# Bidirectional DeltaNet scan on one core: the inverse's product in the other PSUM bank, output sums one step later, square-root chains as steps of VectorE's list

## The chip, the cores and the metric

The kernel runs on one core of one Trainium2 chip. The metric is device time in microseconds (us) of one execution, taken as the median of several runs. A core has TensorE (PE; its weight loads are listed apart as PEld), VectorE (DVE), ScalarE (ACT), GpSimd (POOL) and SyncE (SP, which issues the DMAs here). PSUM is the memory that TensorE writes its products to; this kernel uses it in tiles of 128 partitions x 512 fp32, one bank each.

## What is computed

One encoder layer over 1024 tokens and 16 learned ones, width 1024, in fp32:

```
h = rmsnorm(x, norm1_w); proj = h @ w_in
q, k, v, z, b, a, sc_b, sc_c, sc_x, gate_a, gate_b = split(proj)
o   = gated_deltanet_bidir(q, k, v, z, b, a, ...)          # 8 heads, d = 128, forward + backward scan
y_a = o @ w_branch_dn
y_b = (sc_b * dwconv3(sc_c * sc_x)) @ w_branch_sc
x  += (sigmoid(gate_a) * y_a + sigmoid(gate_b) * y_b) @ w_out
x  += (silu(h2 @ w_gate) * (h2 @ w_up)) @ w_down           # h2 = rmsnorm(x, norm2_w)
out = rmsnorm(x, final_norm_w)
```

The scan of one head and one direction, chunk after chunk (S is a 128 x 128 state, carried from step to step):

```
def step(S, inp):
    v_new = u_c - w_c @ S
    o_c   = qd_c @ S + qk_c @ v_new
    S     = S * gl_c + kd_c.T @ v_new
```

with `u` and `w` from a triangular solve within each chunk. The outputs of both directions are summed, and then scaled by an inverse root of their mean square.

## The kernel before, in words

The work falls into two stages. The first holds the input projection (8 heads x q, k, v, the short convolution's columns, the gates and z), the convolutions and all of the DeltaNet. The second holds the branch projections, the output projection and the SwiGLU; the change does not touch it.

In the first stage the instruction order of every engine is written out by the kernel itself. The main loop emits the dense projections as single matmuls (`dense_steps`, line 340: three products in a split-fp32 format for each of 8 blocks of the contraction). After each of them it calls `run_streams()` and `pump()`. `run_streams` advances four generators, one each for the decay matrices (`g_decay`), the key products (`g_norm`), the inverse of the chunk's triangular matrix (`g_inv`) and the scan (`g_scan`). A generator yields the time at which it wants to go on. It works these times out in a small planner: `T` holds a clock for each engine, `pe(ns)`, `V(n)` and `A(n)` add what an instruction should cost there, and a stream goes on when `T["pe"]` has reached the time it yielded. So between two products of a scan step there stand as many dense matmuls as the planner thinks are needed to cover the work of VectorE and ScalarE in between. `pump` hands single VectorE instructions out of three lists (`conv`: convolutions, `fs`: the forward substitution of `g_inv`, `norm`: the root chains) while VectorE's clock is at most 700 ns ahead of TensorE's. The engines run what they get strictly in that order; the waits between them are semaphores that are put in from the tiles and banks that the instructions touch. One lock (`take`) keeps the scan and the last part of `g_inv` out of each other's three PSUM banks (`pss`, the `pd` tiles of the profile).

One head has one scan of NC = 8 steps. Step i works on chunk i forwards (d = 0) and on chunk 7 - i backwards (d = 1). It takes two banks, `b1` and `b2`, of four 128 x 128 places each:

- line 806: `b1[:, d]` = kT . S, then line 809: `b2[:, d]` = qT . S (TensorE);
- line 816: `r0[d]` = v - decay . `b1[:, d]` (VectorE);
- line 821: `b1[:, 2 + d]` = NP . r0, the product with the inverse (TensorE);
- lines 828 and 833: `w[d]` and `v2[d]`, two scaled copies each of `b1[:, 2 + d]` (ScalarE);
- line 838: `b1[:, d]` = kn . w over the first product's place (TensorE; not in the last step);
- line 842: `b2[:, 2 + d]` = PQ . v2 (TensorE);
- line 851: the new S from `b1[:, d]` (VectorE);
- lines 860 to 880: the output of each direction into `oacc[c]`. In steps 0 to 3 the chunk is met for the first time: a ScalarE copy of `b2[:, d]` (line 869; line 865 where there is no state yet), then a VectorE sum with `b2[:, 2 + d]` (line 875). In steps 4 to 7 a VectorE multiply and add (line 872), the sum (line 875), and a square with its sum over the row on ScalarE (line 879). Direction 0 comes first in all of it, then direction 1.

Ahead of step 0 the learned tokens give the first state (lines 788 to 796, with the VectorE scaling of line 791 and the product of line 793). After step 7 the function `norm` works out the inverse roots with `rsqrt` (line 141 onwards, eleven small VectorE instructions of 9 columns, lines 145 to 155) and scales the outputs (line 891). The same chain for the keys is `norm_job`. Both put the eleven instructions into VectorE's queue in one go.

Of the kernel before, what the change touches and what calls it, by code (L numbers as in the profile page):

```python
# [8 lines left out]
F32 = mybir.dt.float32  # L9
# [7 lines left out]
P = 128  # L17
# [30 lines left out]
def encoder_layer(ctx: ExitStack, tc: tile.TileContext, x, meta, norm1_w, w_in, w_ba,  # L48
# [225 lines left out]
    def V(n, kind=0):  # L274
        return on("dve", (68 + 1.042 * n, 130 + 1.042 * n, 130 + 0.52 * n)[kind])

    def A(n):
        return on("act", 144 + 0.834 * n)
# [209 lines left out]
    def fs_job(h, fN, fP):  # L488

        for j in range(31):  # L490
# [9 lines left out]
            V(r * n)  # L500
            yield T["dve"] + DEP

    def norm_job(st_, ssk1, cc, ce, he, y, tmp, sk):
        nc.vector.tensor_tensor(out=ce, in0=cc, in1=he, op=ALU.mult)
        V(18)
        yield T["dve"] + DEP
        rsqrt(y, ssk1, tmp)
        [V(9) for _ in range(11)]
        yield T["dve"] + DEP
        nc.vector.tensor_tensor(out=sk, in0=y, in1=ssk1, op=ALU.mult)  # L510
        V(9)

# [244 lines left out]
    def g_scan(h, st_):  # L757
        nonlocal freed
        kq, vT, small, kn, NP, PQ, Pm = (st_[k] for k in ("kq", "vT", "small", "kn", "NP", "PQ", "Pm"))
        kT, qT = kq[:, 0], kq[:, 1]  # L760
        ssk, ssq, rk2, ssk1, y, tmp, sk = (small[:, :, i] for i in range(7))
        cc, ce = small[:, :, 7:9], small[:, :, 9:11]
        sso = small[:, :, 11]
        vS = dn.tile([P, 9, P], F32, tag="vS", name=uid("vS"))
        yield from take("scan")

        def newbank():
            return pss().rearrange("p (a n) -> p a n", a=4)

        for grp in ((8, 0, 7), (1, 2, 3), (4, 5, 6)):  # L770
            pt = newbank()
            for i, c in enumerate(grp):
                if c == 8:
                    transpose(pt[:META, i], vT[:, 0:META])
                else:
                    transpose(pt[:, i], vT[:, cs(c)])
            yield pe(330)
            for i, c in enumerate(grp):
                p = META if c == 8 else P
                nc.scalar.activation(vS[:p, c], pt[:p, i], AF.Copy, scale=sk[:p, c:c + 1])  # L780
                A(P)
        yield T["act"] + HOP

        oacc = [NP[:, c, c // 4] for c in range(NC)]


        bank = newbank()
        mm(bank[:META, 0], Pm, vS[:META, 8], start=True, stop=True)
        yield pe(215)
        w = dn.tile([P, P], F32, tag="w0", name=uid("w"))  # L790
        nc.vector.tensor_scalar(out=w[:META], in0=bank[:META, 0], scalar1=ce[:META, 8, 0:1], scalar2=None, op0=ALU.mult)
        yield V(P, 1)
        mm(bank[:, 1], kn[:META, 8], w[:META], start=True, stop=True)
        yield pe(215)
        S0 = dn.tile([P, P], F32, tag="S0", name=uid("S"), bufs=2)
        nc.vector.tensor_copy(S0, bank[:, 1])
        yield V(P, 1)
        S = [S0, None]
        seen = set()
        for i in range(NC):  # L800
            cd = (i, NC - 1 - i)
            hd = (h, 8 + h)
            act_ = [d for d in range(2) if S[d] is not None]
            b1, b2 = newbank(), newbank()
            for d in act_:
                mm(b1[:, d], kT[:, cs(cd[d])], S[d], start=True, stop=True)
            t = pe(215 * len(act_))
            for d in act_:
                mm(b2[:, d], qT[:, cs(cd[d])], S[d], start=True, stop=True)
            pe(215 * len(act_))  # L810
            yield t
            r0 = [vS[:, cd[0]], vS[:, cd[1]]]
            for d in act_:
                c = cd[d]
                r0[d] = dn.tile([P, P], F32, tag=f"r{d}", name=uid("r0"))
                nc.vector.scalar_tensor_tensor(out=r0[d], in0=b1[:, d], scalar=negEG[:, c, hd[d]:hd[d] + 1], in1=vS[:, c],
                                               op0=ALU.mult, op1=ALU.add)
                t = V(P, 1)
            yield t
            for d in range(2):  # L820
                mm(b1[:, 2 + d], NP[:, cd[d], d], r0[d], start=True, stop=True)  # L821
            yield pe(430)
            w = [None, None]
            v2 = [None, None]
            for d in range(2):
                c = cd[d]
                w[d] = dn.tile([P, P], F32, tag=f"w{d}", name=uid("w"))
                nc.scalar.activation(w[d], b1[:, 2 + d], AF.Copy, scale=ce[:, c, d:d + 1])  # L828
                t = A(P)
            for d in range(2):  # L830
                c = cd[d]
                v2[d] = dn.tile([P, P], F32, tag=f"v2{d}", name=uid("v2"))
                nc.scalar.activation(v2[d], b1[:, 2 + d], AF.Copy, scale=cc[:, c, d:d + 1])
                tv = A(P)
            if i < NC - 1:
                yield t
                for d in range(2):
                    mm(b1[:, d], kn[:, cd[d]], w[d], start=True, stop=True)  # L838
                t = pe(430)
            yield tv  # L840
            for d in range(2):
                mm(b2[:, 2 + d], PQ[:, cd[d], d], v2[d], start=True, stop=True)
            t2 = pe(430)
            if i < NC - 1:
                yield t
                for d in range(2):
                    Sn = dn.tile([P, P], F32, tag=f"S{d}", name=uid("S"), bufs=2)
                    if S[d] is None:
                        nc.vector.tensor_copy(Sn, b1[:, d])
                    else:  # L850
                        nc.vector.scalar_tensor_tensor(out=Sn, in0=S[d], scalar=eGl[:, cd[d], hd[d]:hd[d] + 1],  # L851
                                                       in1=b1[:, d], op0=ALU.mult, op1=ALU.add)
                    t = V(P, 1)
                    S[d] = Sn
            else:
                freed += 1
                yield t2

            for d in range(2):
                c = cd[d]  # L860
                eg = eG[:, c, hd[d]:hd[d] + 1]
                first = c not in seen
                seen.add(c)
                if d not in act_:
                    nc.scalar.copy(oacc[c], b2[:, 2 + d])
                    A(P)
                    continue
                if first:
                    nc.scalar.activation(oacc[c], b2[:, d], AF.Copy, scale=eg)
                    A(P)  # L870
                else:
                    nc.vector.scalar_tensor_tensor(out=oacc[c], in0=b2[:, d], scalar=eg, in1=oacc[c],
                                                   op0=ALU.mult, op1=ALU.add)
                    V(P, 1)
                nc.vector.tensor_tensor(out=oacc[c], in0=b2[:, 2 + d], in1=oacc[c], op=ALU.add)
                V(P)
                if not first:
                    jk = dn.tile([P, P], F32, tag="jk", name=uid("jk"))
                    nc.scalar.activation(jk, oacc[c], AF.Square, accum_out=sso[:, c:c + 1])
                    on("act", 310)  # L880
            yield t


        def norm():
            nc.vector.tensor_scalar(out=ssq, in0=ssq, scalar1=EPS, scalar2=EPS * P, op0=ALU.add, op1=ALU.mult)
            nc.vector.scalar_tensor_tensor(out=sso, in0=sso, scalar=1.0 / P, in1=ssq, op0=ALU.mult, op1=ALU.add)
            rsqrt(y, sso, tmp)
            [V(9) for _ in range(13)]
            yield T["dve"] + DEP
            for c in range(NC):  # L890
                nc.vector.tensor_scalar(out=oacc[c], in0=oacc[c], scalar1=y[:, c:c + 1], scalar2=None, op0=ALU.mult)
                V(P, 2)
                yield T["dve"] + DEP
        lock["scan"] = None
        yield T["act"] + HOP
        job = enqueue("norm", norm())
        while not job.done:
            yield T["pe"] + 300
        yield T["dve"] + HOP
        for c4 in range(2):  # L900
            oT = NP[:, 4 * c4:4 * c4 + 4, 1 - c4]
            pt = newbank()
            for c in range(4):
                transpose(pt[:, c], oacc[4 * c4 + c])
            yield pe(430)
            nc.scalar.copy(oT, pt)
            A(512)
            nc.sync.dma_start(o_d[h][:, c4 * 512:(c4 + 1) * 512].rearrange("p (c t) -> p c t", c=4), oT)
# [868 lines left out]
```

## Time and profile before

| | |
|---|---|
| time, median of 3 runs | 2029.02 us (2028.56 to 2034.96) |
| the profiled execution | 2032.53 us |
| its span, first to last instruction | 2030.8 us |
| granted TensorE clock | 0.998 |
| TensorE busy | 2001.7 us, 99% of the span |
| VectorE busy | 1349.6 us, 66% |
| ScalarE busy | 821.3 us, 40% |
| GpSimd busy | 122.8 us, 6% |

The profile is one execution. Its views are: the page; the groups of instructions by line; the waits (who waited for whom: total us, times, longest); one line's instructions; and the timeline, in which a row gives the start in us, the duration in us, the engine, the line, the operation, output<-inputs and, in brackets, how long the engine was idle before it and what ended that. Matmul ends are modelled, so a product's row can reach into the next one's; the starts are recorded. Each fp32 product of the scan shows as two matmul rows (high and low part), hence x4 for a pair.

### The profile page before, as it was taken

Reading aid. Unit: us, or ns where it says so; the run is one execution under the profiler, and the core shown is the slowest. Engines: PE = TensorE matmul, PEld = TensorE weight load, DVE = VectorE, ACT = ScalarE, POOL = GpSimd, SP = SyncE. Lnnn points to the kernel's source line nnn. Section 1 sums busy time; section 2 is a strip of 40 time slices with the busy share of each in tenths; the row PEclk is TensorE's granted clock in tenths of the full one; section 3 lists DMA queues with packets and bytes.
Section 4 is the critical chain, followed back from the end, with each engine's and each line's share of the span. In section 5 each row is a group of like instructions: output and inputs, shape, how many; then the busy total and the mean of one; then the engine's idle time right before and its main releaser. Section 6 shows DMA issues by size and latency. Waiting matters only on the chain.

```text
span 2030.8 us, 31965 instructions
## 1 busy us (share of the span) xinstructions
PE 2001.7 (99%) x12059; PEld 1726.3 (85%) x12059; DVE 1349.6 (66%) x2966; ACT 821.3 (40%) x1945; POOL 122.8 (6%) x407
## 2 busy tenths in 40 slices
PE   9999999999999999999999999999999999999998
PEld 8998898989898988787888888887888888888887
DVE  6888577888888888663214534458867566656575
ACT  6471353645454545534213212134333333335344
POOL 2002102020202020200000000000000000000000
PEclk9999999999999999999999999999999999999999
DMA  3121222222122122221326733122755354477654
GB/s 141 64 69 58 64 85 57 74 59 73 59 68 64 66 66 78 85 89 58 99 99 209 246 122 128 52 83 99 254 207 218 137 174 166 158 275 244 194 174 167
DMA packets 131409, 247.85 MB, mean 122 GB/s; under 512 B 45045, under 2 KB 54694, under 8 KB 128823
## 3 DMA queue, kind: packets, MB, share of 16 engines
q1 hardware_dynamic: 130679, 244.77, 36.4%
q8 instruction: 94, 1.54, 0.3%
q10 hardware_dynamic: 576, 1.05, 0.1%
q14 instruction: 60, 0.49, 0.1%
HBM read 179.10 MB, written 66.67 MB: 121 GB/s over the span
## 4 chain that ended last, share of the span: by engine, by line
PE 49%; DVE 2%; DMA 1%; ACT 1%; issue 0%; SPq 0%; DVEq 0%; ACTq 0%
PE pd L1517 10%; PE pm L340 6%; PE pe L1517 4%; PE pm L1517 3%; PE pe L135 1%; PE pe L133 1%; PE pe L134 1%; PE pd L135 1%; PE pd L133 1%; PE pd L134 1%; PE pe L1685 1%; PE pe L1684 1%; PE pe L1683 1%; PE pd L1685 1%; PE pd L1684 1%; PE pd L1683 1%
## 5 line engine op out<-in xcount | busy, mean ns | idle before, releaser
L340 PE MATMUL pm<-hTh,wl 128*128 128x512 f32 (+4 forms) x1424 | 495.9, 353 | 0.7 <-DVE wl L944 0.7
L340 PE MATMUL pm<-hTh,wh 128*128 128x512 f32 (+4 forms) x1424 | 495.7, 353 | 0.8 <-ACT ra L433 0.4
L340 PE MATMUL pm<-al,wh 128*128 128x512 f32 (+4 forms) x1424 | 495.5, 353 | 0.0
L340 PEld LDWEIGHTS pm<-hTh,wh 128*128 128x128 f32 x1424 | 266.8, 188 | 19.9 <-issue 1.1
L340 PEld LDWEIGHTS pm<-hTh,wl 128*128 128x128 f32 x1424 | 267.1, 188 | 19.0 <-DVE wl L944 1.9
L340 PEld LDWEIGHTS pm<-al,wh 128*128 128x128 f32 x1424 | 267.0, 188 | 16.9
L944 DVE TENSOR_TENSOR wl<-raw,wh 128x512 fp32r<-128x512 f32 x134 | 90.5, 689 | 84.0 <-ACT wh L947 83.6
L101 DVE TENSOR_TENSOR al<-raw,ring_h 128x1024 fp32r<-128x1024 f32 x73 | 88.8, 1223 | 65.2 <-ACT ring_h L100 64.9
L100 ACT CAST ring_h<-raw 128x1024 fp32r<-128x1024 f32 x73 | 76.8, 1053 | 106.8 <-PE pd L1685 35.3
L362 DVE SCALAR_TENSOR_TENSOR kq<-ra,wc,kq 128x520 f32<-128x520 f32 x128 | 96.9, 757 | 10.7 <-ACT kq L392 8.3
L947 ACT CAST wh<-raw 128x512 fp32r<-128x512 f32 x134 | 78.6, 620 | 13.2 <-PE pm L340 9.6
L100 ACT CAST wh<-raw 128x1024 fp32r<-128x1024 f32 x43 | 45.2, 1050 | 85.8 <-PE pe L134 34.5
L495 DVE TENSOR_TENSOR tm<-fP,fN 128x135 f32<-128x135 f32 (+23 forms) x248 | 72.4, 292 | 4.2
L499 DVE TENSOR_TENSOR fP<-fP,tm 128x135 f32<-128x135 f32 (+23 forms) x248 | 71.9, 290 | 4.6
L828 ACT ACTIVATE w<-pd,small 128x128 f32<-128x128 f32 x128 | 40.1, 365 | 82.0 <-PE pd L821 67.0
L1519 DVE TENSOR_TENSOR b<-pd,b 128x512 f32<-128x512 f32 x22 | 15.2, 690 | 68.3 <-PE pd L1517 68.3
L1620 ACT ACTIVATE b<-b 128x512 f32<-128x512 f32 x22 | 13.9, 632 | 115.0 <-DVE b L1519 115.0
L101 DVE TENSOR_TENSOR wl<-raw,wh 128x1024 fp32r<-128x1024 f32 x43 | 52.4, 1220 | 11.1 <-ACT wh L100 10.9
L665 POOL TENSOR_TENSOR tm<-mP,mN 1x15 f32<-1x15 f32 (+7 forms) x120 | 44.5, 371 | 203.3 <-DMA mN<-ndm 194.8
L851 DVE SCALAR_TENSOR_TENSOR S<-S,eGl,pd 128x128 f32<-128x128 f32 x104 | 31.6, 342 | 36.1 <-PE pd L838 18.1
L1517 PE MATMUL pd<-b_hl,wh 128*128 128x512 f32 x176 | 54.3, 390 | 0.0
L533 ACT ACTIVATE PQ<-PQ,negG 128x128 f32<-128x128 f32 x128 | 43.0, 394 | 17.8 <-DVE PQ L528 17.8
(523 smaller groups left out, 4426.5 us busy)
## 6 DMA issues: line engine op xcount, KB each, us to landing
raw<-in_w_in_dram SPq DMA_DIRECT2D x72, 512.0 KB
raw<-in_w_gate_up_dram SPq DMA_DIRECT2D x44, 512.0 KB
sums<-in_w_down_dram SPq DMA_DIRECT2D x22, 512.0 KB
t_d<-sums SPq DMA_DIRECT2D x11, 1024.0 KB
raw<-s_d SPq DMA_DIRECT2D x44, 256.0 KB
raw<-t_d SPq DMA_DIRECT2D x44, 256.0 KB
act_d<-b SPq DMA_DIRECT2D x43, 256.0 KB
raw<-act_d SPq DMA_DIRECT2D x33, 256.0 KB
```

Source lines behind the costliest of these rows:

```text
L100: nc.scalar.copy(hi, src)
L101: nc.vector.tensor_tensor(out=lo, in0=src, in1=hi.bitcast(F32), op=ALU.subtract)
L133: mm(po[:m, :n], wh[:, k, :m], xhk[:, t0:t0 + n], start=(k == 0), stop=False)
L340: mm(po[:, :n], ww[:, k], f(k)[:, t0:t0 + n], start=i == 0, stop=i == 3 * KT - 1)
L362: nc.vector.scalar_tensor_tensor(out=acc, in0=raw[:, h0 + t:h0 + t + hn], scalar=wc[:, t, col:col + 1], in1=acc, op0=ALU.mult, op1=ALU.add)
L495: nc.vector.tensor_tensor(out=tv, in0=fP[:, 0:r, j:j + 1].broadcast_to([P, r, n]), in1=fN[:, j:j + 1, j + 1:32].broadcast_to([P, r, n]), o ...
L499: nc.vector.tensor_tensor(out=fP[:, 0:r, j + 1:32], in0=fP[:, 0:r, j + 1:32], in1=tv, op=ALU.subtract)
L533: nc.scalar.activation(PQ[:, c, d], PQ[:, c, d], AF.Exp, bias=negG2[:, c, hd:hd + 1])
L665: nc.gpsimd.tensor_tensor(out=tv, in0=mP[:, 0:j + 1, j:j + 1].broadcast_to([1, j + 1, n]), in1=mN[:, j:j + 1, j + 1:META].broadcast_to([1, ...
L944: nc.vector.tensor_tensor(out=u[1][1][:, k], in0=u[2][:, k], in1=u[1][0][:, k].bitcast(F32), op=ALU.subtract)
L947: nc.scalar.copy(u[1][0][:, k], u[2][:, k])
L1517: mm(po, x[:, k], y, start=k + i == 0 and not add_to, stop=k == 3 and i == 2, skip_group_check=add_to)
```

## The change

The product with the inverse goes to `b2[:, 2 + d]`, the place that PQ . v2 takes later in the same step; `w` and `v2` are copied from there. The code of the outputs becomes a function. At the end of a step it issues only the copies (or multiply-adds) of `b2[:, d]`, for both directions one after the other. The sums with `b2[:, 2 + d]`, and the squares behind them, are kept in a list and issued in the next step, straight behind the two `r0` instructions; those of the last step follow after a yield behind it. The root chains become a generator that hands out one VectorE instruction at a time, each with a cost and a ready time in the planner; the two instructions ahead of the chain in `norm` are handed out singly too. The arithmetic and the numbers of instructions are the same.

```
+    def rsqrt_steps(y, a, tmp):
+        v = nc.vector
+        ops = [lambda: v.tensor_scalar(out=y.bitcast(I32), in0=a.bitcast(I32), scalar1=1, scalar2=None, op0=ALU.logical_shift_right),
+               lambda: v.tensor_scalar(out=y.bitcast(I32), in0=y.bitcast(I32), scalar1=-1, scalar2=0x5F3759DF,
+                                       op0=ALU.mult, op1=ALU.add)]
+        ops += 3 * [lambda: v.tensor_tensor(out=tmp, in0=y, in1=y, op=ALU.mult),
+                    lambda: v.scalar_tensor_tensor(out=tmp, in0=tmp, scalar=-0.5, in1=a, op0=ALU.mult, op1=ALU.mult),
+                    lambda: v.scalar_tensor_tensor(out=y, in0=tmp, scalar=1.5, in1=y, op0=ALU.add, op1=ALU.mult)]
+        for f in ops:
+            f()
+            V(9)
+            yield T["dve"] + DEP
 ...
-        rsqrt(y, ssk1, tmp)
-        [V(9) for _ in range(11)]
-        yield T["dve"] + DEP
+        yield from rsqrt_steps(y, ssk1, tmp)
 ...
+        pending = []
+        def outputs():
+            while pending:
+                pending.pop(0)()
+
+        def output(b2, c, d, sums):
+            eg = eG[:, c, (h, 8 + h)[d]:(h, 8 + h)[d] + 1]
+            first = c not in seen
+            seen.add(c)
+            if not sums:
+                nc.scalar.copy(oacc[c], b2[:, 2 + d])
+                A(P)
+                return
+            if first:
+                nc.scalar.activation(oacc[c], b2[:, d], AF.Copy, scale=eg)
+                A(P)
+            else:
+                nc.vector.scalar_tensor_tensor(out=oacc[c], in0=b2[:, d], scalar=eg, in1=oacc[c],
+                                               op0=ALU.mult, op1=ALU.add)
+                V(P, 1)
+            def add_up():
+                nc.vector.tensor_tensor(out=oacc[c], in0=b2[:, 2 + d], in1=oacc[c], op=ALU.add)
+                V(P)
+                if not first:
+                    jk = dn.tile([P, P], F32, tag="jk", name=uid("jk"))
+                    nc.scalar.activation(jk, oacc[c], AF.Square, accum_out=sso[:, c:c + 1])
+                    on("act", 310)
+            pending.append(add_up)
 ...
+            outputs()
             yield t
             for d in range(2):
-                mm(b1[:, 2 + d], NP[:, cd[d], d], r0[d], start=True, stop=True)
+                mm(b2[:, 2 + d], NP[:, cd[d], d], r0[d], start=True, stop=True)
 ...
-                nc.scalar.activation(w[d], b1[:, 2 + d], AF.Copy, scale=ce[:, c, d:d + 1])
+                nc.scalar.activation(w[d], b2[:, 2 + d], AF.Copy, scale=ce[:, c, d:d + 1])
 ...
-                nc.scalar.activation(v2[d], b1[:, 2 + d], AF.Copy, scale=cc[:, c, d:d + 1])
+                nc.scalar.activation(v2[d], b2[:, 2 + d], AF.Copy, scale=cc[:, c, d:d + 1])
 ...
             for d in range(2):
-                c = cd[d]
-                eg = eG[:, c, hd[d]:hd[d] + 1]
 ...
-                nc.vector.tensor_tensor(out=oacc[c], in0=b2[:, 2 + d], in1=oacc[c], op=ALU.add)
-                V(P)
 ...
+                output(b2, cd[d], d, d in act_)
             yield t
+        yield t2
+        outputs()
 ...
         def norm():
             nc.vector.tensor_scalar(out=ssq, in0=ssq, scalar1=EPS, scalar2=EPS * P, op0=ALU.add, op1=ALU.mult)
+            V(9)
+            yield T["dve"] + DEP
             nc.vector.scalar_tensor_tensor(out=sso, in0=sso, scalar=1.0 / P, in1=ssq, op0=ALU.mult, op1=ALU.add)
-            rsqrt(y, sso, tmp)
-            [V(9) for _ in range(13)]
+            V(9)
             yield T["dve"] + DEP
+            yield from rsqrt_steps(y, sso, tmp)
```

More of the change, by code (lines that the diff above doesn't have):

```diff
@@ L859, in g_scan @@
             for d in range(2):
-                c = cd[d]
-                eg = eG[:, c, hd[d]:hd[d] + 1]
[L862 to L875, printed above, removed]
-                V(P)
[L877 to L880, printed above, removed]
+                output(b2, cd[d], d, d in act_)
             yield t
+        yield t2
+        outputs()
         def norm():
             nc.vector.tensor_scalar(out=ssq, in0=ssq, scalar1=EPS, scalar2=EPS * P, op0=ALU.add, op1=ALU.mult)
+            V(9)
+            yield T["dve"] + DEP
             nc.vector.scalar_tensor_tensor(out=sso, in0=sso, scalar=1.0 / P, in1=ssq, op0=ALU.mult, op1=ALU.add)
-            rsqrt(y, sso, tmp)
-            [V(9) for _ in range(13)]
+            V(9)
             yield T["dve"] + DEP
+            yield from rsqrt_steps(y, sso, tmp)
             for c in range(NC):
```

## The prediction

> **What bounds the kernel now.** I read the page first, then the main product's line, then the waits, and then the timeline of single scan steps.
>
> ```profile
> span 2030.8 us, 31965 instructions
> ...
> PE 2001.7 (99%) x12059; PEld 1726.3 (85%) x12059; DVE 1349.6 (66%) x2966; ACT 821.3 (40%) x1945; POOL 122.8 (6%) x407
> ...
> L340 PE MATMUL pm<-hTh,wh x1424: 302/334/586, 16.3 to 1081.7; 128*128 128x512 f32 x58, 128*128 128x320 f32 x40, 128*128 128x384 f32 x40, 128*128 128x336 f32 x24
> ...
> L891 DVE TENSOR_SCALAR NP<-NP,small x64: 277/281/289, 278.7 to 974.2; 128x128 f32<-128x128 f32 x64
> ```
>
> TensorE sets the time. Its first stage, where the scans run, reaches to the last dense product at 1081.7 us. The last head's outputs are scaled at 974.2, so the streams end 107 us before their cover does. What the change can give or cost is therefore TensorE time lost in waits of that stage. The waits that bear on the edited lines:
>
> ```profile
> ACT jk L879 <- DVE NP L875: 67.7, 57, 3.0
> ...
> PEld pd L838 <- ACT v L833: 17.5, 45, 0.6
> ...
> DVE NP L875 <- ACT NP L869: 15.3, 39, 0.5
> ...
> PEld pd L821 <- DVE r L816: 8.0, 18, 1.0
> ...
> PEld pd L793 <- DVE w L791: 2.9, 5, 1.0
> ...
> PE pd L821 <- DVE r L816: 2.6, 7, 0.7
> ...
> PE pe L590 <- DVE PQ L617: 2.1, 4, 0.8
> ...
> PE pd L793 <- DVE w L791: 1.5, 4, 0.7
> ...
> L838 PE MATMUL pd<-w,kn 128*128 128x128 f32 x224 | 39.0, 297 | 3.2 <-ACT v L833 0.5
> ...
> L821 PE MATMUL pd<-r,NP 128*128 128x128 f32 x240 | 38.8, 281 | 2.9 <-DVE r L816 2.6
> ```
>
> The telling row is the second: the product kn.w (line 838) reads `w` and never `v`, yet its weight load waits 45 times for the copies into `v`. Here is one step in order of time, from the sums of the step before to PQ.v2:
>
> ```profile
> 441.42 0.28 DVE L875 TENSOR_TENSOR NP<-pd,NP 128x128 f32<-128x128 f32 x1
> ...
> 441.74 0.37 ACT L869 ACTIVATE NP<-pd,eG 128x128 f32<-128x128 f32 x1 [0.50 <-DVE NP L875]
> ...
> 442.14 0.29 DVE L875 TENSOR_TENSOR NP<-pd,NP 128x128 f32<-128x128 f32 x1 [0.44 <-ACT NP L869]
> ...
> 442.35 0.31 DVE L495 TENSOR_TENSOR tm<-fP,fN 128x31 f32<-128x31 f32 x1
> ...
> 442.58 0.75 DVE L362 SCALAR_TENSOR_TENSOR kq<-ra,wc,kq 128x520 f32<-128x520 f32 x1
> ...
> 443.25 0.60 DVE L816 SCALAR_TENSOR_TENSOR r<-pd,negEG,vS 128x128 f32<-128x128 f32 x2
> ...
> 443.31 0.33 PE L340 MATMUL pm<-al,wh 128*128 128x384 f32 x1
> ...
> 443.48 0.34 PE L340 MATMUL pm<-hTh,wl 128*128 128x384 f32 x1
> ...
> 443.90 0.52 PEld L821 LDWEIGHTS pd<-r,NP 128*128 128x128 f32 x4 [0.40 <-DVE r L816]
> ...
> 444.70 0.63 ACT L828 ACTIVATE w<-pd,small 128x128 f32<-128x128 f32 x2 [0.64 <-PE pd L821]
> ...
> 445.21 0.63 ACT L833 ACTIVATE v<-pd,small 128x128 f32<-128x128 f32 x2
> ...
> 445.44 0.32 PE L340 MATMUL pm<-hTh,wh 128*128 128x336 f32 x1
> ...
> 445.60 0.31 PE L340 MATMUL pm<-al,wh 128*128 128x336 f32 x1
> ...
> 445.89 0.52 PEld L838 LDWEIGHTS pd<-w,kn 128*128 128x128 f32 x4 [0.26 <-ACT v L833]
> ...
> 446.60 0.61 PE L842 MATMUL pd<-v,PQ 128*128 128x128 f32 x4
> ```
>
> Dense products start 0.16 us apart (445.44, 445.60), and the next start is 445.89: 0.29. So 0.13 of a wait of 0.26 is lost, and the other half lies under the product in flight. In the same way line 821's load waits 0.40 and TensorE loses 443.90 - 443.48 - 0.17 = 0.25.
>
> **Part 1, the inverse's product in `b2`.** `w` is complete at 444.70 + 0.63 = 445.33, `v` at 445.21 + 0.63 = 445.84. The load goes at 445.89, right behind `v`. The only link is that kn.w writes the bank that the `v` copies are still reading, at other columns. With NP.r0 in `b2` the copies read `b2`, kn.w has `b1` to itself, and what it waits for is `w`. Its natural start is 445.60 + 0.16 = 445.76, 0.43 behind `w`: the wait goes, and nothing is late in its place in such a step. Its size: 17.5 on PEld and 0.5 on PE, 18.0 us in 47 waits, 0.38 each. Lower bound is the 3.2 us of PE's own idle column; upper bound takes off only the hidden 0.13 of the step shown, 18.0 - 47 x 0.13 = 11.9. Wider dense products hide more, and half of each wait, as in the step shown, is 9.0. I take **9.0**. The Trainium skill ("PSUM — Partial Sum Buffer", section "PSUM bank collisions raise a hardware error") says that a different address of the same bank collides as well, so that accesses of two engines are put in order bank by bank; the rows above agree.
>
> **Part 2, sums one step later, copies in front.** Now the first-visit steps run back and forth: sum, copy, sum, copy (441.42 to 442.35), and VectorE stands idle 0.44 in it; over all heads it is 15.3 us in 39 waits. In VectorE's strict order this lies ahead of the next `r0`. From 441.42 to 442.35 that is 0.93 us; the lost time at line 821 is 0.25. With the sums behind `r0`, `r0` comes up to 0.93 earlier, bounded by its product kT.S, and the stall goes. Total for line 821: 8.0 + 2.6 = 10.6 us of waits in 25; half to 0.25/0.40 of it is 5.3 to 6.6 lost, at least the 2.9 of the idle column. I take 5.3, of which **4.2** (four fifths) goes: convolution steps of 0.75 alone can still hold up some `r0`. What is late next is the new S (line 851), now behind two sums of 0.29, but kn.w, which it needs, comes over 2 us after `r0` (443.85 to 445.89). Banks: the sums read a `b2` that is next written two steps later, which is behind the next S in VectorE's own order.
>
> **Part 3, the squares.** The squares of steps 4 to 6 move with the sums, and now stand on ScalarE ahead of the next step's `w` and `v`:
>
> ```profile
> L879 ACT ACTIVATE jk<-NP x64: 309/310/312, 256.1 to 968.7; 128x128 f32<-128x128 f32 x64
> L879 ACT ACTIVATION_READ_ACCUMULATOR jk<-NP x64: 185/187/203, 256.4 to 968.9; 128x1 f32 x64
> ```
>
> One takes 0.31 + 0.19 = 0.50. Put into the step above: `r0` ends 443.85, the sums 444.14 and 444.43, the squares 444.64 and 445.14, and `w` starts at 445.14 instead of 444.70, 0.44 late. The cover of kn.w is 0.43, that of PQ.v2 is 446.60 - 0.13 - 445.84 = 0.63. So it just fits. It concerns steps 5 and 6 for kn.w and 5 to 7 for PQ.v2, 16 and 24 places. No row of before shows it; bounds are 0 (no gain: only the root chain reads the squares) and 16 x 0.4 = 6.4. I take a **cost of 1.5**, about 0.04 a place, since the cover works out just even.
>
> **Part 4, the root chains in steps.**
>
> ```profile
> 634.92 0.18 DVE L153 SCALAR_TENSOR_TENSOR small<-small 128x9 f32<-128x9 f32 x1
> ...
> 635.13 0.18 DVE L155 SCALAR_TENSOR_TENSOR small<-small 128x9 f32<-128x9 f32 x1
> ...
> 635.34 0.43 DVE L641 STREAM_TRANSPOSE NP<-NP 32x256 f32<-32x256 f32 x1
> ...
> 636.76 0.31 PE L340 MATMUL pm<-al,wh 128*128 128x320 f32 x1
> 636.94 0.34 DVE L791 TENSOR_SCALAR w<-pd,small 16x128 f32<-16x128 f32 x1
> ...
> 637.33 0.37 PE L793 MATMUL pd<-w,kn 16*128 16x128 f32 x1 [0.26 <-DVE w L791]
> ```
>
> One of the eleven takes 0.21 from start to start (634.92, 635.13), the chain 2.3 us. The planner books 68 + 9.4 = 77 ns each, 0.85 us, so it sends what follows 1.5 us too early; the product at 637.33 comes 0.57 behind a dense one that takes about 0.15. In steps each is booked at 77 + 127 = 204 ns, about what it takes, with other work let in between. Line 793 waits 2.9 + 1.5 = 4.4 us; the lost part is between 1.5 (PE's own) and half of both, 2.2. I take 1.8, of which **1.3** goes, since the transposes ahead of line 791 stay. No VectorE work is added. The chain gets longer, and the order of the changed program shows it: the last head's output transposes stand 160 TensorE instructions later, with 317 left before the stage's last dense product. At up to 0.23 us each, 37 of the 107 us of cover are used. This costs nothing while cover is left.
>
> No DMA or queue of SP or POOL is added. The planner's list re-sorts some units (heads 3 and 5 to 7 come a few units later), so waits outside the edit, like line 590's 2.1, fall elsewhere: 2 us either way.
>
> **The sum.** 9.0 + 4.2 + 1.3 - 1.5 = 13.0 us. The profiled execution, 2032.53 us (span 2030.8 and 1.7 around it), would take 2019.5. The median of the runs shown is 3.5 lower, 2029.02, and gives **2016.0**. What a measurement here can tell from no change is about 0.3%, 6.1 us, that is 2022.9. By the bounds: at most 11.9 + 6.6 + 2.2 + 2 = 22.7 (2006), at least 3.2 + 2.9 + 1.5 - 6.4 - 2 = -0.8.
>
> **The rivals.** (a) *The wait only moves.* NP.r0 and PQ.v2 now share two places of `b2`, so the first PQ.v2 must wait for both `v` copies, where it has nothing left to wait for today since kn.w waited before it. If kn.w's loss came back there, 4.2 + 1.3 - 1.5 = 4.0 would remain: 2025. The Trainium skill's page on PSUM, in the same section, gives the rule behind it: order by bank, not by address. Against: without the stall PQ.v2 starts at 446.47, and `v` ends at 445.84, 0.63 before. Chance 0.07.
>
> (b) *The loss isn't there.* Ends are modelled; if only what PE's column names as released by these lines is real (0.5 + 2.6 + 1.5 = 4.6), the time is 2024.4. For it: 99% busy. Against: starts are recorded, and 0.29 stands where 0.16 is the rhythm. Chance 0.10.
>
> (c) *Slower: the squares hold up `w`.* Place: ScalarE, steps 5 to 7 of every head. Sums and squares wait for each other 67.7 us in 57 waits now. If the pair ends 1.0 later than worked out, `w` is 1.44 late, kn.w loses 1.0 at 16 places and PQ.v2 0.8 at the 8 last steps, 22.4 us against a gain of 14.5: 2037. It decides from 0.6 us of lateness beyond the cover on, where 24 x 0.6 eats the gain. Against: both sums are issued straight behind `r0`, and wait for nothing. Chance 0.07.
>
> **How the numbers follow.** Forecast 0.74, (a) 0.07, (b) 0.10, (c) 0.07, and 0.02 for a re-sorted order that loses over 6 us. The range 2008 to 2026 holds the forecast with its bounds short of the last 2 us, and (a) and (b). Faster by over 0.3%: the forecast, and a little of (b): 0.76. Within 0.3%: the rest of (a) and (b), and a weak form of (c): 0.15. Slower: 0.09.
>
> **What would show it.** In the changed profile no row of kn.w waiting for `v`, at most a few us for `w`; VectorE's sums no longer waiting for line 869's copy; line 821's waits for `r` under 3 us, line 793's near 2; line 842 with waits for `v` under 2 us; TensorE's stage ending about 13 us earlier, at 1069. It is wrong if line 842 or the `w` waits take up more than 5 us, or if the dense products' last start stays at 1080.

## The result, and the profile after

The changed kernel took 2005.9 us (median of 5 runs, 2003.49 to 2007.57) against 2030.92 for the kernel before in the same comparison (5 runs, 2028.56 to 2034.96): a ratio of 0.9875, 95% interval 0.986 to 0.989. That is 25.0 us less, where 13.0 were forecast; 2005.9 lies below the forecast range, which began at 2008. The profiled execution took 2006.06 us.

The page, and the line of the dense product, whose last start marks the end of the first stage:

```profile
span 2004.3 us, 31913 instructions
...
PE 1985.3 (99%) x12059; PEld 1730.0 (86%) x12059; DVE 1334.7 (67%) x2966; ACT 816.9 (41%) x1945; POOL 116.5 (6%) x407
...
L340 PE MATMUL pm<-hTh,wh x1424: 302/334/586, 16.7 to 1056.0; 128*128 128x512 f32 x58, 128*128 128x320 f32 x40, 128*128 128x384 f32 x40, 128*128 128x336 f32 x24
```

The stage ends at 1056.0 instead of 1081.7, 25.7 us sooner; so the whole gain arose there. TensorE is as "busy" as before, 99%: the share told nothing of it. The scan's products by line (line 883 is the former 838, 866 the former 821, 887 the former 842, 850 the former 806), and the waits of weight loads and matmuls at these lines:

```profile
L850 PE MATMUL pd<-S,kq 128*128 128x128 f32 x240 | 37.9, 277 | 1.0 <-DVE S L896 0.8
...
L866 PE MATMUL pd<-r,NP 128*128 128x128 f32 x240 | 37.2, 274 | 0.0
...
L883 PE MATMUL pd<-w,kn 128*128 128x128 f32 x224 | 34.0, 274 | 0.0
```

```profile
PEld pd L850 <- DVE S L896: 2.6, 6, 0.9
...
PEld pd L887 <- ACT v L878: 0.2, 1, 0.2
...
PEld pd L866 <- DVE r L860: 0.2, 1, 0.2
```

Line 883 has no wait left for `v`, nor one for `w`; line 866 waits 0.2 us in all, where 10.6 stood; line 887, where rival (a) saw the wait come back, has 0.2. One step of a chunk's second visit, in order of time:

```profile
450.83 0.61 DVE L860 SCALAR_TENSOR_TENSOR r<-pd,negEG,vS 128x128 f32<-128x128 f32 x2 [0.23 <-PE pd L850]
...
451.36 0.48 DVE L836 TENSOR_TENSOR NP<-pd,NP 128x128 f32<-128x128 f32 x2
...
451.67 0.31 ACT L840 ACTIVATE jk<-NP 128x128 f32<-128x128 f32 x1 [2.89 <-DVE NP L836]
...
452.32 0.19 ACT L840 ACTIVATION_READ_ACCUMULATOR jk<-NP 128x1 f32 x1
452.34 0.17 DVE L506 TENSOR_SCALAR small<-small 128x9 int32<-128x9 int32 x1
452.43 0.75 DVE L362 SCALAR_TENSOR_TENSOR kq<-ra,wc,kq 128x520 f32<-128x520 f32 x1
452.47 0.61 PE L866 MATMUL pd<-r,NP 128*128 128x128 f32 x4
...
453.09 0.17 DVE L507 TENSOR_SCALAR small<-small 128x9 int32<-128x9 int32 x1
...
453.11 0.63 ACT L873 ACTIVATE w<-pd,small 128x128 f32<-128x128 f32 x2 [0.60 <-PE pd L866]
...
453.63 0.63 ACT L878 ACTIVATE v<-pd,small 128x128 f32<-128x128 f32 x2
...
454.10 0.32 PE L340 MATMUL pm<-hTh,wl 128*128 128x336 f32 x1
454.11 0.56 PEld L883 LDWEIGHTS pd<-w,kn 128*128 128x128 f32 x4
...
454.26 0.61 PE L883 MATMUL pd<-w,kn 128*128 128x128 f32 x4
```

Here every part can be seen. The sums (line 836) stand behind `r0`. The squares (line 840) are over at 452.51, and ScalarE then idles 0.60 until line 866 is through: they hold up nothing. The root chain (lines 506, 507) lets a convolution step in between. Line 883's load runs at 454.11, 0.15 ahead of its product, while the `v` copies are still at work until 454.26.

### The profile page after: what moved, and what is told of

It reads as the page before. It is cut to its first block, busy times and chain, and to the rows that moved or that the text cites. A ratio compares the mean times of both kernels' runs of the same rounds, so it can differ in the third digit from the quotient of the medians.

```text
span 2004.3 us, 31913 instructions
## 1 busy us (share of the span) xinstructions
PE 1985.3 (99%) x12059; PEld 1730.0 (86%) x12059; DVE 1334.7 (67%) x2966; ACT 816.9 (41%) x1945; POOL 116.5 (6%) x407
## 4 chain that ended last, share of the span: by engine, by line
PE 68%; DVE 5%; DMA 1%; ACT 1%; issue 1%; SPq 0%; DVEq 0%; ACTq 0%
PE pm L340 19%; PE pd L1546 10%; PE pe L1546 4%; PE pm L1546 3%; PE pe L133 1%; PE pe L134 1%; PE pe L135 1%; PE pd L133 1%; PE pd L135 1%; PE pd L134 1%; PE pe L1713 1%; PE pe L1712 1%; PE pe L1714 1%; PE pd L1713 1%; PE pd L1712 1%; PE pd L1714 1%
## 5 line engine op out<-in xcount | busy, mean ns | idle before, releaser
L860 DVE SCALAR_TENSOR_TENSOR r<-pd,negEG,vS 128x128 f32<-128x128 f32 x120 | 36.7, 345 | 26.5 <-PE pd L850 26.5
L840 ACT ACTIVATE jk<-NP 128x128 f32<-128x128 f32 x64 | 19.9, 311 | 81.8 <-DVE NP L836 80.8
```

## The experiments

Times are medians; each is compared with runs of the kernel before that were made beside it. For the reading of a trace I use one count beside the views: the *late start* of a group of products, which is its start less the start of the last dense product ahead of it, less the median distance between two dense starts of that width (0.227 us for 512 columns, 0.174 for 384, 0.154 for 336, 0.150 for 322, 0.147 for 320), and less 0.087 where that dense product stands alone between two groups. These are sums over the first stage. A group of kn.w or NP.r0 is the pair for both directions.

**The other bank alone.** No order of instructions changes.

```
-                mm(b1[:, 2 + d], NP[:, cd[d], d], r0[d], start=True, stop=True)
+                mm(b2[:, 2 + d], NP[:, cd[d], d], r0[d], start=True, stop=True)
   (and w[d], v2[d] copied from b2[:, 2 + d])
```

> The kernel before with the product with the inverse in the step's other bank alone; every engine's instruction order stays as before. Theory A (a wait costs the pair's late start and, on top, about 0.10 us inside the stalled pair, because its second weight load could not run ahead): line 838 loses its 9.2 us of late starts and 5.0 us in the pairs, so 14 us less, about 2017; the mean of a line 838 row falls from 297 to 275 ns; line 821 stays near 281 ns and its 10.6 us of waits. Theory B (the prediction's term: only the late starts count): 9 us less, about 2022.

2019.44 us against 2031.40, ratio 0.994 (0.9927 to 0.9952): 12.0 less. Groups of this kernel, and its waits for S:

```profile
L821 PE MATMUL pd<-r,NP 128*128 128x128 f32 x240 | 39.4, 284 | 1.8 <-DVE r L816 1.3
...
L838 PE MATMUL pd<-w,kn 128*128 128x128 f32 x224 | 34.0, 274 | 0.0
```

```profile
PEld pd L806 <- DVE S L851: 2.8, 9, 0.7
```

The time lies between Theory A's 2017 and Theory B's 2022. Theory A holds for line 838: its late starts fall from 9.5 to 0.2, and the time inside the pairs (from first to last start of a pair's rows, summed) from 23.6 to 18.6. Those 14.3 us are not the whole account: 2.5 came back at kT.S, which now waits for S (late starts 0.5 to 1.9, inside the pairs 19.7 to 20.8). That TensorE reaches the next step sooner, and VectorE is not there yet, is my reading of it. Each bank is one tile here, so no run tells whether the order that made kn.w wait goes by the tile or by the bank.

**The root chains alone.**

```
-        rsqrt(y, ssk1, tmp)
-        [V(9) for _ in range(11)]
-        yield T["dve"] + DEP
+        yield from rsqrt_steps(y, ssk1, tmp)
   (and the same in norm())
```

> The kernel before with the root chains handed out singly, nothing else. Theory A: line 793's late starts go (1.6 us) and some of what stands behind a chain; 1.5 to 3 us less, about 2028.5. Rival: the re-sorted order is what gave the change its unpredicted 3.1 us at line 590, and it comes with these steps: 5 us less or more, about 2026. Lines 838 and 821 keep their waits (within 2 us of 18.0 and 10.6).

2028.50 against 2031.40, ratio 0.9984 (0.9975 to 0.9993): 2.9 less. The first product after the learned tokens loses 0.8 instead of 2.5, and the key products of line 590 lose 1.5 instead of 3.2. This is the size that Theory A gave, and not the rival's 5 us.

**The sums alone.** One step later, copies in front, with the first bank and the chains in one go.

```
+            outputs()                      # behind the two r0 of the next step
             yield t
 ...
+                output(b2, cd[d], d, d in act_)
```

> The kernel before with the output sums one step later and the copies in front, nothing else. Theory A: line 821's waits go, 5.3 us of late starts and 1.6 us in the pairs, so 7 us less, about 2024, and line 838 keeps its waits for the v copies. The prediction's terms: 4.2 gained and 1.5 lost to the squares ahead of w and v, 2.7 us less, about 2028, with longer waits at line 838.

2029.81 against 2031.40, ratio 0.9994 (0.9985 to 1.0003): not to be told from no change by itself. The groups of line 821 and 838 (here 868 and 885):

```profile
L885 PE MATMUL pd<-w,kn 128*128 128x128 f32 x224 | 39.1, 297 | 3.4 <-ACT v L880 0.9
...
L868 PE MATMUL pd<-r,NP 128*128 128x128 f32 x240 | 37.7, 277 | 1.4 <-DVE r L862 1.3
```

The late starts at the product with the inverse fall from 5.3 to 2.5 (6 stalled groups instead of 15). Two of the six, 0.67 and 0.74 us, have two convolution steps of 0.76 directly ahead of `r0`, one of 0.23 has a root chain ahead of it. Line 885 waits as before, with 17.2 us: the squares, now ahead of `w`, made nothing longer. Neither expectation holds: Theory A's 7 us did not come, and the time fits the prediction's terms without the longer waits at line 838 that they asked for.

**The wait covered instead of removed.** kn.w is handed out when the planner thinks `v` is complete.

```
             if i < NC - 1:
-                yield t
+                yield tv
                 for d in range(2):
                     mm(b1[:, d], kn[:, cd[d]], w[d], start=True, stop=True)
```

> The kernel before, with kn.w handed out when the planner thinks v is complete instead of w (one yield changed), the bank as before. If what counts is only that TensorE arrives at kn.w before the v copies are over: the waits at line 838 go without any change of banks, its rows fall to 275 ns, 12 to 14 us less, about 2017. If the shared bank itself costs something beside the wait: less than half of that, 2024 or above.

2022.10 against 2031.40, ratio 0.9954 (0.9942 to 0.9967): 9.3 less. Line 838 falls to 274 ns and 0.2 us of late starts with both matmuls in the old bank. So the shared bank cost nothing beyond the wait at this line. The time, 2022.1, is 5 above what I expected for that case and 2 below the rival's 2024, so it does not decide by itself; the line's own figures do. Of the 5, the re-sorted order lost 2.7 at line 821 (late starts 8.0) and 1.6 at kT.S.

**Parts in pairs.** Three kernels, in this order: bank and sums (the chains in one go); bank and chains (the sums in their old place); sums and chains (the old bank).

> The changed kernel with the root chains in one go as before: other bank and late sums. Theory A (the three parts add up; what is missing from the whole is chance of the re-sorted order): 12.0 + 1.6 less than before, about 2017.5. Theory B (bank and sums need each other: with the wait at line 838 gone TensorE comes to the next steps sooner, so r0 and S have to be early too): 20 us less or more, about 2010, and the stalls of the product with the inverse under 1 us. Theory C (sums and root chains need each other, both being VectorE work ahead of r0): about 2017, with 2 us or more of late starts left at the product with the inverse.

> Other bank and root chains in steps, sums as before. Theory A: 12.0 + 2.9 less than before, about 2016.5, with some 4 us of late starts left at the product with the inverse. Theory B: the same. Theory C: the same. If the gap to the whole lies between these two parts instead: about 2009.

> The changed kernel with the product with the inverse back in the first bank: late sums and root chains in steps. Theory A and B: 1.6 + 2.9 less than before, about 2027, and line 838's equivalent with about 18 us of waits for v, its rows at 297 ns. Theory C: 10 us less or more, about 2021, with no late starts left at the product with the inverse.

2015.07, 2015.64 and 2019.84 against 2032.18; ratios 0.9918 (0.9904 to 0.9931), 0.9918 (0.9904 to 0.9931) and 0.9941 (0.9928 to 0.9953). By the times it is Theory C on this list: sums and chains together give 12.3 us, alone 1.6 and 2.9. The bank adds 12.7 to that (25.0 less 12.3), as it did by itself. Late starts and time inside the pairs, in us (the last row takes every dense product, hence 1082.1 and 1056.4 where the groups shown end at 1081.7 and 1056.0):

| | before | changed | bank | roots | sums | bank, sums | bank, roots | sums, roots |
|---|---|---|---|---|---|---|---|---|
| NP.r0, late | 5.3 | 0.2 | 4.0 | 5.2 | 2.5 | 1.5 | 4.1 | 0.5 |
| NP.r0, inside | 23.0 | 21.4 | 23.5 | 23.6 | 21.9 | 21.7 | 23.3 | 21.4 |
| kn.w, late | 9.5 | 0.2 | 0.2 | 9.7 | 9.7 | 0.1 | 0.2 | 9.5 |
| kn.w, inside | 23.6 | 18.6 | 18.6 | 23.5 | 23.7 | 18.6 | 18.6 | 23.4 |
| kT.S, late | 0.5 | 2.1 | 1.9 | 1.7 | 1.7 | 3.1 | 3.1 | 0.6 |
| keys (590), late | 3.2 | 1.2 | 3.5 | 1.5 | 3.4 | 3.5 | 2.3 | 1.2 |
| tokens (793), late | 2.5 | 0.8 | 2.5 | 0.8 | 1.5 | 1.5 | 0.8 | 0.7 |
| dense, late | 10.4 | 8.1 | 9.9 | 8.6 | 10.0 | 9.7 | 8.3 | 8.1 |
| last dense start | 1082.1 | 1056.4 | 1070.5 | 1077.5 | 1079.3 | 1066.4 | 1064.9 | 1069.2 |

On this list the stalls of NP.r0 vanish only where both sums and chains are changed (0.2 and 0.5). Sums and chains together exceed the sum of their parts by 7.8 us. The table puts 3.0 of that at NP.r0 (1.9 late, 1.1 inside) and 2.3 at kT.S, which lost 1.2 in each part alone. The reason that Theory C gives, the root chains as work ahead of `r0`, is not shown: of the six stalls left under the sums alone, one had a chain ahead of it, and the second list below speaks against it. The two rows of sums and roots without the bank show the two terms side by side:

```profile
L883 PE MATMUL pd<-w,kn 128*128 128x128 f32 x224 | 38.8, 296 | 3.5 <-ACT v L878 1.1
...
L866 PE MATMUL pd<-r,NP 128*128 128x128 f32 x240 | 37.2, 275 | 0.1
```

**A longer wait.** The kernel before without the yield ahead of kn.w, so that every one of the 56 pairs stalls.

```
             if i < NC - 1:
-                yield t
                 for d in range(2):
                     mm(b1[:, d], kn[:, cd[d]], w[d], start=True, stop=True)
```

> The kernel before with the yield ahead of kn.w taken out, so that kn.w stands directly behind the product with the inverse's copies in the planner's order and always arrives before v is complete: a longer wait at each of 56 pairs. If a stalled pair costs its late start and a fixed 0.10 us inside: the rows of line 838 rise only to about 299 ns (56 stalled pairs instead of 39 to 47), the late starts from 9.5 to 45 us or more, and the time by as much as the late starts, 2065 or above. If the loss inside the pair grew with the wait, the rows would go to 330 ns or more.

2096.04 against 2032.18, ratio 1.0315 (1.0296 to 1.0334): 63.9 more. The group and its wait:

```profile
L837 PE MATMUL pd<-w,kn 128*128 128x128 f32 x224 | 39.9, 301 | 58.0 <-ACT v L833 58.0
```

```profile
PEld pd L837 <- ACT v L833: 74.6, 56, 2.6
```

The waits are four times as long (74.6 us against 17.5), the rows only 4 ns longer. Late starts rise from 9.5 to 66.1; inside the pairs it is 24.5 against 18.6 without a stall, 5.9 over 56 stalled pairs, 0.105 each. The loss inside a stalled pair is fixed. The starts in the trace show what it is. In each of the 56 pairs the second weight load starts 107 to 110 ns behind the first, and its product 105 to 108 behind that. In the changed kernel, where no pair stalls, the second load starts 1 or 2 ns behind the first product. I read the loss as one weight load, some 0.1 us, that no product covers.

**Is it the order's chance?** Four kernels with one neutral change, which re-sorts the first stage widely and so gives a second list: before, sums, sums and chains, and the changed kernel.

```
-            pe(n / 2.4 + 13)
+            pe(n / 2.4 + 14)
```

> The kernel before with one neutral change of the planner, a dense matmul booked 1 ns dearer, which re-sorts the order of the first stage widely without taking out or adding anything. If re-sorting alone is worth little: within 3 us of the kernel before, 2028 to 2035. If the 7 us that sums and root chains brought together beyond their own parts are chance of the order: scatter of 5 us or more between this and the kernel before.

> Late sums and copies in front alone, with the same neutral change of the planner. Theory C (sums need the root chains in steps): again 1 to 3 us less than the kernel before. If it is chance: anywhere between 0 and 12 us less.

> Late sums and root chains in steps, first bank as before, with the same neutral change of the planner. Theory C: again 10 to 13 us less than the kernel before, near 2020. If it is chance: about 4.5 us less, 2027.

> The changed kernel with the same neutral change of the planner. If the 25 us are the change's own: 2003 to 2009. If some 7 of them are chance of the order: 2010 to 2014.

2039.27, 2034.25, 2028.01 and 2015.63 against 2031.24; ratios 1.0039 (1.0024 to 1.0054), 1.0016 (1.0006 to 1.0025), 0.9983 (0.9974 to 0.9993) and 0.9921 (0.9906 to 0.9936). Each is 4 to 10 us slower than the same kernel on the first list, so my expectations, which compare across lists, missed. On the new list, against its own kernel before: sums 5.0, sums and chains 11.3, the whole change 23.6. So the whole and the two big blocks (bank 12.4, sums and chains 11.3) stay; how the second block splits (sums alone 5.0 here, 1.6 there) depends on the order. The chains alone were not run on this list. What the traces do show is the product with the inverse, before and with the sums alone:

```profile
L821 PE MATMUL pd<-r,NP 128*128 128x128 f32 x240 | 39.1, 283 | 3.2 <-DVE r L816 2.9
```

```profile
L868 PE MATMUL pd<-r,NP 128*128 128x128 f32 x240 | 37.5, 276 | 0.0
```

Its late starts fall from 6.2 to 0.3 with the chains still in one go, and stay at 0.8 with sums and chains. So the stalls of NP.r0 do not need the chains in steps; Theory C's mechanism fails here. What the chains add on this list, 6.2 us, lies elsewhere: 1.9 at the learned tokens' product, 1.6 at kn.w, 0.9 at the keys, and some 5 in dense products, less what kT.S and NP.r0 lost (1.7 and 0.5). Whether all four got slower by chance, or because a dearer dense matmul lets the planner put a little less cover between two products, stays open.

**Copies in front without the later step.** The changed kernel with the sums at the end of their own step, behind both copies.

```
-            outputs()                      # behind the two r0
 ...
                 output(b2, cd[d], d, d in act_)
+            outputs()
```

> The changed kernel with the sums issued at the end of the same step again, behind both copies, so that of part 2 only the copies in front are left. If the gain at the product with the inverse comes from ending the back and forth between the sums and the copies: about as the changed kernel, within 3 us of 2006, with under 1 us of late starts there. If it comes from taking the sums out of the way of r0: 2012 to 2016, with 2 to 4 us of late starts there, as in the kernel with the other bank and the root chains alone.

2008.71 against 2031.46, ratio 0.9892 (0.9875 to 0.9908). Its product with the inverse:

```profile
PEld pd L865 <- DVE r L860: 2.4, 3, 1.0
```

2.0 us of late starts, between the 4.1 of bank and chains and the 0.2 of the changed kernel. The time is within 3 us of the changed kernel, as the first expectation had it; the late starts are those of the second. So both steps count: ending the back and forth between sums and copies took 2.1 us of late starts, putting the sums behind `r0` took 1.8. Each step re-sorts the list as well, so this split is no firmer than the scatter above.

**Convolution steps booked dearer.** The changed kernel, with 110 ns more in the planner for each convolution step.

```
                 V(hn, 1)
+                T["dve"] += 110
                 yield T["dve"] + DEP
   (and the same in the short convolution)
```

> The changed kernel with each convolution step on VectorE booked 110 ns dearer in the planner (672 ns booked, some 790 from start to start in the trace). If what is left of late r0 and S comes from convolution steps booked too cheaply: the waits for the new S at the product of kT and S (2.6 us on the loads, 0.8 on the matmuls) go nearly to nothing, 1 to 4 us less than the changed kernel. If it is only another order: anywhere within 10 us, as the neutral change of the planner showed, with such waits still there.

2009.00 against 2031.46, ratio 0.9892 (0.9877 to 0.9907): not faster than the changed kernel. Two rows of it:

```profile
L852 PE MATMUL pd<-S,kq 128*128 128x128 f32 x240 | 37.7, 277 | 0.2
```

```profile
PEld pd L807 <- DVE w L805: 2.4, 1, 2.4
```

The waits for S at kT.S are fewer (0.8 us of late starts instead of 2.1), but a single wait of 2.4 at the learned tokens' product stands in their place. That fits the cause named, and does not show it: in the changed kernel kT.S lost 2.1 on the first list and 4.5 on the second, so a new order alone moves it by as much.

## Why the prediction was wrong, point by point

The places that it names were right, and so was the reason for the wait at line 838; the sum was half the size, 13.0 instead of 25.0. The step that failed first of all: the loss behind a wait was taken to be how late the pair starts, and what a stalled pair loses inside was put at nothing. That loss was 5.0 at line 838 and 1.6 at line 821, over half of the 12.0 missed. The runs split it another way: the bank alone gave 12.0 where 9.0 were forecast, and the other three parts together 12.3 where their sum was 4.0. By the prediction's own terms, with the stalled product's row in the step that the prediction shows:

```profile
445.90 0.71 PE L838 MATMUL pd<-w,kn 128*128 128x128 f32 x4
```


- **Part 1, forecast 9.0, measured 14.3 at its line and 12.0 in the time.** "Half of each wait, as in the step shown, is 9.0" was taken as the whole loss. I counted how late the pair starts (9.0; measured 9.3, a close hit from a share read off one step, which owes something to luck) and not what happens inside it. A stalled pair runs 0.71 us (the row above), one without a stall 0.60 or 0.61 (the changed kernel at 454.26). The row that I quoted held it: line 838 with a mean of 297 ns, where 274 or 275 is the rule; 224 rows x 22 ns are 4.9 us. My upper bound of 11.9 lacked it too. The bank alone and the longer wait show it as a term of its own, fixed at 0.10 a pair.
- **Part 2, forecast 4.2, measured 6.7 in the changed kernel.** All of the late starts at NP.r0 went (5.1 of 5.3), and 1.6 inside its pairs, the same neglected term: 281 ns in the row that I quoted. "Four fifths" was too little. The sums alone took 2.8 of the late starts on this list and 5.9 of 6.2 on the second, so whether the sums suffice depends on the order, which the prediction did not weigh.
- **Part 3, forecast a cost of 1.5, measured nothing.** I put the squares into a step with a stalled NP.r0, where `w` follows `r0` by 0.85 (443.85 to 444.70). Where NP.r0 isn't stalled the distance is longer, 1.67 in the step shown (451.44 to 453.11), and the squares also overlap the second sum.
- **Part 4, forecast 1.3, measured 1.7 at line 793** (2.5 to 0.8 of late starts). What I booked as "2 us either way" was a gain: late starts at line 590 fell by 2.0, and those of dense products by 2.3; some of these waited for weights that VectorE splits (line 944, waits of 1.9 on the loads and 0.7 on the products, none in the changed kernel). Both are lower in each kernel with the chains in steps than in its counterpart without. That it is the chain's burst of 2.3 us which held these up is argued, not shown by itself.
- **"Nothing is late in its place" failed in a small way.** S is late next: kT.S lost 1.6 more in late starts and 0.6 inside its pairs. In four of its six late groups a convolution step of 0.7 to 0.8 us stands directly ahead of S in VectorE's list.

The terms of the changed kernel add up: 14.3 + 6.7 + 1.7 + 2.0 + 2.3 - 2.2 = 24.8, of 25.7 at the stage's end. Rival (a) is refuted by line 887's 0.2 us. Rival (b), the loss by PE's idle column, was the farthest from the truth: the column held 3.2 where 14.3 were to be had. Rival (c) is refuted by the sums alone, where line 838's equivalent waited no longer than before. The cover at the end of the stage was enough, as said.

The range failed with the sum: its lower end was put inside my own upper bound for the gain, and that bound missed the pairs.

On the load: the Trainium skill ("TensorE: Matmul & The Clock Gate", section "Step-by-step: what each phase is for") says that weights for the next tile load while the present matmul runs. The trace agrees where nothing waits: the load starts at 454.11, 0.15 ahead of its product at 454.26. Where the load carries the wait, the two start 0.01 apart (445.89 and 445.90), and the pair takes 0.10 longer.

## What to carry to other kernels

When a product waits on something it does not read, look for whose access of the same PSUM bank it is put behind, and give the two a bank each; handing the product out later also took the wait away here (9.3 us against 12.0). Size a TensorE stall by three things: the late start, the group's mean duration against its unstalled sisters, and what the next engine will be late with; the idle column of an engine that is "99% busy" is no bound. In a schedule written from a planner's costs, compare variants on more than one list: a booking changed by 1 ns moved these kernels by 4 to 10 us. The gain of the whole and of the bank held within 1.5 us; that of the sums alone did not (1.6 and 5.0), and the reason found for it on one list failed on the other.

## What was not expected of the hardware

A stalled pair of fp32 products loses a fixed 0.10 us inside, whatever the length of its wait: 213 ns between its first two starts in the 47 pairs of the kernel before whose load waited for `v`, 108 to 114 in eight of the other nine, and 0.105 a pair with waits of 1.3 us each (74.6 us in 56). VectorE's 128 x 520 convolution steps follow each other at 0.79 us or so (an instruction shows as 0.75 to 0.76), where the planner books 0.67.
